# A softmax on one core: seven tiles of up to 31 rows in one written-out queue, in place of twelve of up to 15

## The chip, the cores and the metric

The kernel runs on one core of one Trainium2 chip. The metric is the device time of one execution in microseconds (us); the median of three runs is given. A profile belongs to one further execution, whose own time stands beside it.

## The reference

```python
x = np.random.randn(16, 1024, 512).astype(np.float32)

def reference(x):
    x_scaled = x / 2.0
    x_max = np.max(x_scaled, axis=-1, keepdims=True)
    exp_x = np.exp(x_scaled - x_max)
    return (exp_x / np.sum(exp_x, axis=-1, keepdims=True)).astype(np.float32)
```

A softmax with temperature 2 over the last axis of 512 values, for 16,384 vectors. 33.55 MB are read and 33.55 MB are written.

## The kernel before

The vectors are spread over the 128 partitions, so each partition has 128 vectors. In this document a *row* is one vector on each of the 128 partitions: 128 x 512 x 4 B = 262,144 B. There are 128 rows to load and 128 to store.

All data lives in one buffer in SBUF, `arena`, of 100 rows, and is worked on in place. `PLAN` (L11) lists the tiles: for each, the sizes of its chunks in rows and the place in the arena where it begins. A tile is the unit of transfer, a chunk the unit of computing. A tile of r rows is laid out so that each partition's share is contiguous in DRAM: one descriptor carries r x 2,048 B. Here there are 12 tiles of 3, 7, 15, 15, 15, 15, 15, 15, 15, 7, 3 and 3 rows; a tile of 15 rows has descriptors of 30,720 B and three chunks of 5 rows. The first eight tiles fill the arena (3 + 7 + 6 x 15 = 100 rows). The last four reuse places of earlier tiles, and `behind` (L63) lists for each which stores must have landed before it may be loaded.

Each chunk k goes through four steps:

- `do_max(k)` on VectorE (L86): the negated maximum of each vector, for the whole chunk in one instruction, once the tile's load has landed (`ld[t]`).
- ScalarE (L112): for each row one `activation`, exp of half the value plus the bias, with the sum of the vector as a second output.
- `do_mul(k)` on VectorE (L95, L99): the reciprocals of the sums in one instruction, and then one multiplication per row.
- `s_mul` counts the chunks that are finished, and a tile is stored when its last one is.

VectorE runs its instructions in the order written, which the loop at L125 sets: do_max(0), do_max(1), do_max(2), do_mul(0), do_max(3), do_mul(1), and so on, `LAG` = 2 chunks apart.

All transfers are issued by SyncE on one queue. `issue_loads` issues the eight loads that wait for nothing, two of them ahead of the start barrier of the program. Then SyncE stores tile after tile, waiting for `s_mul` at L133, and puts the four late loads between stores; these wait at L138 for the landing of the stores that they overwrite. At the end SyncE waits for every store (L141):

```python
        for t in range(len(tiles)):
            nc.sync.wait_ge(st[t], 16)
```

After that comes the closing barrier of all engines, with GpSimd gathering them. GpSimd itself has four small memsets at the start and no other work.

Of the kernel before, what the change touches and what calls it, by code (L numbers as in the profile page):

```python
# [1 line left out]

# [4 lines left out]

PLAN = [  # L11
    ([3], 0), ([4, 3], 3), ([5] * 3, 10), ([5] * 3, 25), ([5] * 3, 40), ([5] * 3, 55),
    ([5] * 3, 70), ([5] * 3, 85), ([5] * 3, 10), ([4, 3], 3), ([3], 0), ([3], 25),
]
ARENA = 100
LAG = 2


@with_exitstack
def kernel(  # L20
    ctx: ExitStack,
    tc: tile.TileContext,
    x: bass.AP,
    out: bass.AP,
):
    nc = tc.nc
    fp32 = mybir.dt.float32

    xf = x.flatten_outer_dims()
    of = out.flatten_outer_dims()  # L30
    N, D = xf.shape
    P = nc.NUM_PARTITIONS
    n_rows = N // P
    assert sum(sum(c) for c, _ in PLAN) == n_rows

    arena = nc.alloc_sbuf_tensor("arena", (P, ARENA, D), fp32)
    negmax = nc.alloc_sbuf_tensor("negmax", (P, n_rows), fp32)
    sums = nc.alloc_sbuf_tensor("sums", (P, n_rows), fp32)
    recip = nc.alloc_sbuf_tensor("recip", (P, n_rows), fp32)

    tiles, chunks, base = [], [], 0
    for t, (cs, at) in enumerate(PLAN):
        r = sum(cs)
        tiles.append((base, r, at))
        o = 0
        for c in cs:
            chunks.append((t, base + o, c, at + o))
            o += c  # L50
        base += r
    last_chunk = {c[0]: k for k, c in enumerate(chunks)}

    def dram(ap, t):
        b, r, _ = tiles[t]
        return ap[b * P : (b + r) * P].rearrange("(p r) d -> p r d", r=r)

    def sb(t):
        _, r, at = tiles[t]
        return arena[:, at : at + r, :]  # L60


    behind = {}  # L63
    for t, (_, r, at) in enumerate(tiles):
        for u in range(t):
            _, ru, au = tiles[u]
            if at < au + ru and au < at + r:
                behind.setdefault(t, []).append(u)

    ld = [tc.alloc_semaphore(f"ld{t}") for t in range(len(tiles))]  # L70
    st = [tc.alloc_semaphore(f"st{t}") for t in range(len(tiles))]
    s_max = tc.alloc_semaphore("s_max")
    s_exp = tc.alloc_semaphore("s_exp")
    s_rec = tc.alloc_semaphore("s_rec")
    s_mul = tc.alloc_semaphore("s_mul")

    def issue_loads(begin, end):
        for t in range(begin, end):  # L80
            if t not in behind:
                nc.sync.dma_start(out=sb(t), in_=dram(xf, t)).then_inc(ld[t], 16)

    def do_max(k):
        t, b, c, a = chunks[k]
        nc.vector.reduce_max(  # L86
            out=negmax[:, b : b + c],
            in_=arena[:, a : a + c],
            axis=mybir.AxisListType.X,
            negate=True,  # L90
        )._wait_ge(ld[t], 16).then_inc(s_max, 1)

    def do_mul(k):
        t, b, c, a = chunks[k]
        nc.vector.reciprocal(  # L95
            out=recip[:, b : b + c], in_=sums[:, b : b + c]
        )._wait_ge(s_exp, k + 1).then_inc(s_rec, 1)
        for r in range(c):
            ins = nc.vector.tensor_scalar_mul(  # L99
                out=arena[:, a + r],  # L100
                in0=arena[:, a + r],
                scalar1=recip[:, b + r : b + r + 1],
            )
            if r == 0:
                ins._wait_ge(s_rec, k + 1)
        ins.then_inc(s_mul, 1)

    def compute_and_store():

        for k, (t, b, c, a) in enumerate(chunks):  # L110
            for r in range(c):
                ins = nc.scalar.activation(  # L112
                    out=arena[:, a + r],
                    in_=arena[:, a + r],
                    func=mybir.ActivationFunctionType.Exp,
                    bias=negmax[:, b + r : b + r + 1],
                    scale=0.5,
                    accum_out=sums[:, b + r : b + r + 1],
                )
                if r == 0:  # L120
                    ins._wait_ge(s_max, k + 1)
            ins.then_inc(s_exp, 1)


        for k in range(len(chunks) + LAG):  # L125
            if k < len(chunks):
                do_max(k)
            if k >= LAG:
                do_mul(k - LAG)

        late = sorted(behind)
        for t in range(len(tiles)):
            nc.sync.wait_ge(s_mul, last_chunk[t] + 1)  # L133
            nc.sync.dma_start(out=dram(of, t), in_=sb(t)).then_inc(st[t], 16)
            while late and max(behind[late[0]]) <= t - 1:
                u = late.pop(0)
                for v in behind[u]:
                    nc.sync.wait_ge(st[v], 16)  # L138
                nc.sync.dma_start(out=sb(u), in_=dram(xf, u)).then_inc(ld[u], 16)
        for t in range(len(tiles)):  # L140
            nc.sync.wait_ge(st[t], 16)  # L141

    hook = nc.inst_callbacks[-1]
    nc.remove_inst_callback(hook)
    symbolic = nc._always_lower_symbolic_ap
    nc._always_lower_symbolic_ap = False
    here = str(nc.cur_bb)
    entry = nc.main_func.blocks[0]  # L150
    head, jumps = entry.instructions[:-5], entry.instructions[-5:]
    entry.instructions = []
    nc.switch_bb("main", None)
    issue_loads(0, 2)
    first = list(entry.instructions)
    at = next(k for k, i in enumerate(head) if type(i).__name__ == "InstDrain")
    entry.instructions = head[:at] + first + head[at:]
    issue_loads(2, len(tiles))
    compute_and_store()
    entry.instructions = list(entry.instructions) + jumps  # L160
    nc.switch_bb(here, None)
    nc._always_lower_symbolic_ap = symbolic
    nc.push_inst_callback(hook)


# [1 line left out]
_INS = ['x']  # L167
_OUTS = [((16, 1024, 512), 'float32')]


# [23 lines left out]
```

The softmax here doesn't subtract the row's maximum and nothing guards it: scores larger than these inputs give would overflow.

## Time and profile before

| what | value |
|---|---|
| median of 3 runs | 163.73 us (163.58 to 163.92) |
| profiled execution, its own time | 163.36 us |
| its span, first to last instruction | 161.6 us |
| VectorE busy | 126.1 us, until 137.9 us |
| ScalarE busy | 94.5 us |
| share of the 16 DMA engines | 97.7% of the span |
| moved | 67.14 MB, mean 416 GB/s |
| DMA packets of the kernel's queue | 3,456 |

The span is counted from the first instruction that the profiler records to the last; the execution's own time has some 1.8 us around it. The page gives the span in 40 slices of 4.04 us: a digit is the busy share of an engine in tenths, and the line of GB/s says what the DMA engines moved. The 3,456 packets are 24 transfers of 128 descriptors (3,072), and 16 small ones for each transfer (384), which count its landing up. A reduction in VectorE's timeline with "<-DMA" behind it stood waiting for a load, so that its start says when that load could be used.

### The profile page before, as it was taken

What the parts mean: (1) busy time and instruction counts of PE and PEld (TensorE: products, weight loads), DVE (VectorE), ACT (ScalarE), POOL (GpSimd) and SP (SyncE); (2) the same over time, 40 slices, a digit from 0 to 9 for tenths busy, and PEclk for the clock granted to TensorE, in tenths of its full rate; (3) what the DMA queues carried; (4) which work ended last, traced back from release to release, by engine and by line L of the source; (5) the groups of instructions that cost most, each with busy time, mean ns of one, the idle gap of its engine ahead of it and who ended that gap; (6) DMA issues with size and microseconds to landing.
All of it is one profiled execution on the core that took longest, in us unless ns stands there. A gap on an engine that the chain in (4) does not pass through costs nothing.

```text
span 161.6 us, 513 instructions
## 1 busy us (share of the span) xinstructions
DVE 126.1 (78%) x184; ACT 94.5 (59%) x257; POOL 0.2 (0%) x4
## 2 busy tenths in 40 slices
DVE  0484599999999999999999999999999999100000
ACT  3439087866688666797666886667978655000000
POOL 0000000000000000000000000000000000000000
DMA  7999999999999997999999899999999999999992
GB/s 291 465 403 449 441 418 464 395 458 395 464 411 436 449 411 254 444 438 472 418 434 464 388 431 406 445 456 388 461 441 456 395 464 395 464 411 456 390 410 90
DMA packets 3460, 67.14 MB, mean 416 GB/s; under 512 B 385, under 2 KB 385, under 8 KB 1153
## 3 DMA queue, kind: packets, MB, share of 16 engines
q1 hardware_dynamic: 3456, 67.11, 97.7%
q14 instruction: 4, 0.02, 0.0%
HBM read 33.55 MB, written 33.55 MB: 415 GB/s over the span
## 4 chain that ended last, share of the span: by engine, by line
DVE 74%; DMA 10%; issue 0%; DVEq 0%
DVE negmax L86 40%; DVE arena L99 32%; DMA arena<-in_x_dram 10%; DVE recip L95 2%; DVEq L189 0%
## 5 line engine op out<-in xcount | busy, mean ns | idle before, releaser
L112 ACT ACTIVATE arena<-arena,negmax 128x512 f32<-128x512 f32 x128 | 90.7, 710 | 40.1 <-DVE negmax L86 40.1
L86 DVE TENSOR_REDUCE negmax<-arena 128x5 f32<-128x2560 f32 (+2 forms) x28 | 72.3, 2586 | 10.8 <-DMA arena<-in_x_dram 10.8
L99 DVE TENSOR_SCALAR arena<-arena,recip 128x512 f32<-128x512 f32 x128 | 53.2, 482 | 1.0
L112 ACT ACTIVATION_READ_ACCUMULATOR arena<-arena,negmax 128x1 f32 x128 | 23.9, 187 | 0.0
L95 DVE RECIPROCAL recip<-sums 128x5 f32<-128x5 f32 (+2 forms) x28 | 5.0, 177 | 0.0
L112 ACT ACT_TABLE_LOAD x1 | 1.3, 1283 | 1.3 <-PEq L178 1.3
L178 POOL MEMSET const-bfloat16-1.0<- 128x1 bf16 x1 | 0.1, 101 | 0.0
L178 POOL MEMSET const-uint8-127<- 128x1 uint8 x1 | 0.1, 101 | 0.0
L178 POOL MEMSET const-float32-0.0<- 128x1 f32 x1 | 0.1, 98 | 0.2 <-issue 0.2
L178 POOL MEMSET const-float32-1.0<- 128x1 f32 x1 | 0.1, 98 | 0.0
## 6 DMA issues: line engine op xcount, KB each, us to landing
arena<-in_x_dram SPq DMA_DIRECT2D x7, 3840.0 KB, 33.7
out_dram<-arena SPq DMA_DIRECT2D x7, 3840.0 KB, 33.2
arena<-in_x_dram SPq DMA_DIRECT2D x2, 1792.0 KB, 15.2
out_dram<-arena SPq DMA_DIRECT2D x2, 1792.0 KB, 33.2
arena<-in_x_dram SPq DMA_DIRECT2D x3, 768.0 KB, 23.5
out_dram<-arena SPq DMA_DIRECT2D x3, 768.0 KB, 22.6
```

The source lines that it names most:

```text
L86: nc.vector.reduce_max(out=negmax[:, b : b + c], in_=arena[:, a : a + c], axis=mybir.AxisListType.X, negate=True,)._wait_ge(ld[t], 16).the ...
L95: nc.vector.reciprocal(out=recip[:, b : b + c], in_=sums[:, b : b + c])._wait_ge(s_exp, k + 1).then_inc(s_rec, 1)
L99: ins = nc.vector.tensor_scalar_mul(out=arena[:, a + r], in0=arena[:, a + r], scalar1=recip[:, b + r : b + r + 1],)
L112: ins = nc.scalar.activation(out=arena[:, a + r], in_=arena[:, a + r], func=mybir.ActivationFunctionType.Exp, bias=negmax[:, b + r : b + r ...
L178: nc = _bacc.Bacc("TRN2", target_bir_lowering=False, num_devices=1)
```

## The change

`PLAN` has seven tiles of 7, 15, 31, 31, 15, 22 and 7 rows, and 22 chunks of 3 to 8 rows in place of 28 of 3 to 5. The arena has 99 rows; the first five tiles fill it (7 + 15 + 31 + 31 + 15). A row share of 31 rows is a descriptor of 63,488 B. Tile 5 (22 rows) takes the places of tiles 0 and 1, tile 6 (7 rows) a part of that of tile 2.

The order of transfers is written out in `QUEUE`, and `do_queue` issues it on SyncE as it stands: a load waits for the stores in `behind`, a store for `s_mul`. Load 5 stands after store 2, load 6 after store 3. The first two loads (`EARLY`) go out ahead of the start barrier, as before.

Stores that a later load waits for (0, 1 and 2) keep a semaphore each; the others share `s_end`. The last wait is on GpSimd: four waits, for stores 0, 1, 2 and for `s_end`.

```diff
 PLAN = [
-    ([3], 0), ([4, 3], 3), ([5] * 3, 10), ([5] * 3, 25), ([5] * 3, 40), ([5] * 3, 55),
-    ([5] * 3, 70), ([5] * 3, 85), ([5] * 3, 10), ([4, 3], 3), ([3], 0), ([3], 25),
+    ([4, 3], 0), ([5] * 3, 7), ([8, 8, 8, 7], 22), ([8, 8, 8, 7], 53), ([5] * 3, 84),
+    ([6, 6, 5, 5], 0), ([4, 3], 22),
 ]
-ARENA = 100
+ARENA = 99
 LAG = 2
+QUEUE = [
+    ("load", 0), ("load", 1), ("load", 2), ("load", 3), ("load", 4),
+    ("store", 0), ("store", 1), ("store", 2), ("load", 5), ("store", 3), ("load", 6),
+    ("store", 4), ("store", 5),
+    ("store", 6),
+]
+EARLY = 2
...
+    awaited = {u for us in behind.values() for u in us}
...
-    st = [tc.alloc_semaphore(f"st{t}") for t in range(len(tiles))]
+    st = {t: tc.alloc_semaphore(f"st{t}") for t in sorted(awaited)}
+    s_end = tc.alloc_semaphore("s_end")
...
-    def issue_loads(begin, end):
-        for t in range(begin, end):
-            if t not in behind:
+    stored = {}
+
+    def do_queue(items):
+        for kind, t, *rest in items:
+            if kind == "load":
+                for u in behind.get(t, []):
+                    nc.sync.wait_ge(st[u], stored[u])
                 nc.sync.dma_start(out=sb(t), in_=dram(xf, t)).then_inc(ld[t], 16)
+                continue
+            lo, hi, groups = rest if rest else (0, tiles[t][1], [(0, P)])
+            b, r, at = tiles[t]
+            k = max(k for k, c in enumerate(chunks) if c[0] == t and c[1] - b < hi)
+            nc.sync.wait_ge(s_mul, k + 1)
+            for p, q in groups:
+                u = t if t in awaited else "end"
+                nc.sync.dma_start(
+                    out=dram(of, t)[p:q, lo:hi], in_=arena[p:q, at + lo : at + hi, :]
+                ).then_inc(st[t] if t in awaited else s_end, 16)
+                stored[u] = stored.get(u, 0) + 16
...
-        late = sorted(behind)
-        for t in range(len(tiles)):
-            nc.sync.wait_ge(s_mul, last_chunk[t] + 1)
-            nc.sync.dma_start(out=dram(of, t), in_=sb(t)).then_inc(st[t], 16)
-            while late and max(behind[late[0]]) <= t - 1:
-                u = late.pop(0)
-                for v in behind[u]:
-                    nc.sync.wait_ge(st[v], 16)
-                nc.sync.dma_start(out=sb(u), in_=dram(xf, u)).then_inc(ld[u], 16)
-        for t in range(len(tiles)):
-            nc.sync.wait_ge(st[t], 16)
...
-    issue_loads(0, 2)
+    do_queue(QUEUE[:EARLY])
...
-    issue_loads(2, len(tiles))
-    compute_and_store()
+    do_compute()
+    do_queue(QUEUE[EARLY:])
+
+    for u, sem in [*st.items(), ("end", s_end)]:
+        nc.gpsimd.wait_ge(sem, stored[u])
```

## The prediction

> **What bounds the kernel now.** I read the busy shares and slices of the page first, then the chain.
>
> ```profile
> DVE 126.1 (78%) x184; ACT 94.5 (59%) x257; POOL 0.2 (0%) x4
> ...
> DVE  0484599999999999999999999999999999100000
> ...
> DMA  7999999999999997999999899999999999999992
> GB/s 291 465 403 449 441 418 464 395 458 395 464 411 436 449 411 254 444 438 472 418 434 464 388 431 406 445 456 388 461 441 456 395 464 395 464 411 456 390 410 90
> ...
> q1 hardware_dynamic: 3456, 67.11, 97.7%
> ...
> DVE 74%; DMA 10%; issue 0%; DVEq 0%
> ```
>
> The chain names VectorE for 74%, but VectorE ends at 137.9 us of 161.6, and the last five slices show transfers alone. The queue is full at 97.7%: **bytes set the end**, and VectorE runs just ahead of them. The one hole is slice 16, with 254 GB/s. Windows give its size and the flow around it (columns: length, busy times of VectorE, ScalarE and GpSimd, clock, DMA share, GB/s):
>
> ```profile
> 0.00:1.00 1.00, 0.00 (x0) 0.00 (x0) 0.20 (x4) 1.00 0.00 0
> 1.00:2.00 1.00, 0.00 (x0) 0.74 (x1) 0.00 (x0) 1.00 0.92 264
> ```
>
> ```profile
> 60.00:64.00 4.00, 3.96 (x6) 2.71 (x9) 0.00 (x0) 1.00 0.80 238
> 64.00:100.00 36.00, 35.75 (x53) 26.95 (x75) 0.00 (x0) 1.00 1.01 434
> ```
>
> The hole costs (434 - 238) / 434 x 4 = 1.8 us. Next, the timeline of VectorE, where a reduction starts when its load is usable:
>
> ```profile
> 4.51 1.75 DVE L86 TENSOR_REDUCE negmax<-arena 128x3 f32<-128x1536 f32 x1 [4.51 <-DMA arena<-in_x_dram]
> 8.77 3.95 DVE L86 TENSOR_REDUCE negmax<-arena 128x4 f32<-128x2048 f32 x2 [2.51 <-DMA arena<-in_x_dram]
> 17.88 2.82 DVE L86 TENSOR_REDUCE negmax<-arena 128x5 f32<-128x2560 f32 x1 [3.77 <-DMA arena<-in_x_dram]
> ```
>
> Call a row of all 128 partitions (262,144 B) one row. These lines stand for 3, 10 and 25 rows: (17.88 - 8.77) / 15 = **0.607 us a row** in 30 KB descriptors, (8.77 - 4.51) / 7 = 0.609 in 14 KB ones. The first load took 4.51 - 3 x 0.607 = 2.7 us beside its bytes: 1.0 empty, about 0.4 of slow start (264 GB/s in the second microsecond), the rest landing.
>
> Last, the chain in order of time gives the prices of VectorE (start, us, what):
>
> ```profile
> 31.55 2.73 DVE negmax L86
> 34.27 0.11 DVE recip L95
> 34.38 0.02 issue
> 34.41 2.07 DVE arena L99 x5
> ...
> 120.28 2.19 DVE negmax L86
> ...
> 128.53 1.66 DVE negmax L86
> ...
> 133.77 1.28 DVE arena L99 x3
> ```
>
> A maximum over c rows costs 0.533c + 0.06 us (2.73, 2.19, 1.66 for 5, 4, 3); a scaling with its reciprocal 0.395c + 0.22 (2.20 for 5, 1.41 for 3). Together 0.93 us a row: slower than one transfer, quicker than a load and a store (1.21). So VectorE can't keep up while the queue only loads.
>
> **What the Trainium skill says.** "DMA: Bandwidth & Descriptors", section "Queues, rings and completion order": each DMA engine takes a queue's descriptors in ring order. The trace agrees: the store issued at 14.14 us landed 52.9 us later, behind all eight loads. Section "Where 436 GB/s comes from" puts the ceiling at 435.2 GB/s; 434 above is already there, so larger descriptors have nothing to win in the steady flow. Section "Latency and other measured facts" gives some 0.6 us to the first byte on this kind of queue; the trace has 1.0. No page prices a wait on GpSimd.
>
> **Part 1: descriptors.** Tiles fall from 12 to 7, transfers from 24 to 14. The 14 KB and 30 KB rows differ by 0.002 us. So I price a 62 KB row at 0.607 as well; the bounds are 0.604 (the ceiling) and 5% more, which no row excludes.
>
> **Part 2: the long tile delays VectorE.** Loads 0 to 4 go out at once, as before. Usable: load 0 (7 rows) at 4.51 + 4 x 0.607 = 6.9, load 1 (22 rows) at 8.77 + 12 x 0.607 = 16.1, load 2 (53 rows) at 8.77 + 43 x 0.607 = 34.9. VectorE works in order, and scalings come two chunks late (LAG). From 16.1: maxima of chunks 2, 3, 4 (3 x 2.73) and scalings of chunks 0, 1, 2 (1.80 + 1.41 + 2.20), 13.6 us, to 29.7. The maximum of chunk 5 waits for load 2, and the scalings of chunks 3 and 4, ready to run, stand behind it: 5.2 us idle. VectorE is idle for 5.7 + 5.2 + 5.2 us from 1.2 to 34.9, where before it was 10.8.
>
> **Part 3: store 2 comes too late.** Its wait is for the scaling of chunk 8, which stands after the maximum of chunk 10. From 34.9: maxima of 8, 8, 8, 7, 8, 8 rows = 5 x 4.32 + 3.79 = 25.4 us; scalings of 5, 5, 8, 8, 8, 7 rows = 2 x 2.20 + 3 x 3.38 + 2.99 = 17.5. Sum 42.9, so store 2 is issued at 77.8. ScalarE (5.7 us for 8 rows) has two maxima and a scaling as cover. Store 0 is issued about 25 and store 1 about 48, in time. The queue holds 99 loaded and 22 stored rows: 1.4 + 121 x 0.607 + 1.8 (the hole, if it comes again) = 76.7. Behind store 2 on SyncE stand load 5, store 3 and load 6, so nothing else can fill the queue. A restart costs 1.0 to 1.4 us by the first two windows; I take 1.2. First bytes at 79.0: **2.3 us empty**, 4.1 without the hole. Either way 79.0 holds, since VectorE sets it; here the hole costs nothing.
>
> **Part 4: the second stop.** From 79.0 run store 2, load 5, store 3, load 6: 91 rows, 55.2 us, to 134.2. Store 3's scaling is done at 77.8 + 26.7 = 104.5, before its turn at 79.0 + 53 x 0.607 = 111.2. Load 5 needs stores 0 and 1, load 6 needs store 2; they land long before those turns. Load 6 is usable at 134.2 + 1.1 = 135.3. VectorE, which works on load 5 from 112.3 for 21.7 us, is free at 134.0. Then maximum of 4 rows, scaling of 5, maximum of 3, scaling of 5: 2.28 + 2.20 + 1.66 + 2.20 = 8.3, so store 5 is issued at 143.7. The queue had store 4 (15 rows, 9.1 us) until 143.3. Store 5's bytes begin at 144.9: **1.6 us empty**. Store 6 is ready by 147 and hidden.
>
> **Part 5: the end.** Stores 5 and 6 are 29 rows, 17.6 us, to 162.5. In the kernel before, 1.4 + 256 x 0.607 + 1.8 = 158.6 us of flow stand against 160.5, where SyncE's last wait ended: 1.9 for landing and drift between the DMA engines. Drift restarts at each stop, so I take 0.8 (ends 0.4 and 1.9). From that wait to the end it was 161.6 - 160.5 = 1.1 us. The waits move to GpSimd, behind which nothing is queued but the closing barrier, and SyncE goes to the barrier early. That saves at most the 0.3 us in which SyncE's branch and drain passed; GpSimd could as well be slower by as much; I take -0.1. Span: 162.5 + 0.8 + 1.1 - 0.1 = **164.3**. Semaphores and instructions fall in number, which costs or saves nothing seen.
>
> **Sum.** The profiled execution was 163.36 us, 1.8 beside its 161.6 span, and 0.37 below the median of 163.73. The new span gives 164.3 + 1.8 + 0.4 = **166.5 us**, +2.8.
>
> **Rivals.**
> - **More loss:** 62 KB descriptors cost 5% more, or the hole comes after the first stop. On the path lie 31 long rows before 34.9 and 62 after 79.0, 93 x 0.607 = 56.5 us; 5% is 2.8, the hole 1.8. For it: the hole's cause isn't shown. Against: descriptor size didn't matter from 14 to 30 KB. 168.3 to 169.3.
> - **Cheaper restarts:** 0.6 us each and landings shorter by 0.3, with the barrier's full gain: 166.5 - 1.7 = 164.8. Against: the second at the start shows 1.0.
> - **Faster:** long descriptors lift the rate itself. The 56.5 us would have to fall by 3.2 us, 5.6%, for a gain over 0.3: 0.573 us a row, or 457 GB/s. The windows and the ceiling speak against it. At 6%, 163.1.
> - **It does not do what it says:** a 63,488 B row is cut in two. Then rates are those of 30 KB rows and both stops stay: 166.5.
>
> **Numbers.** Forecast (with the cut rows) 0.68, more loss 0.20, cheaper restarts 0.08, faster 0.04. The forecast itself is good for 165.3 to 167.7. The range reaches from the cheap restarts to the hole uncovered and some drift, 164.8 to 168.8. A measurement here tells about 0.2% (0.33 us) from no change: faster 0.04, same 0.03 (the cheapest restarts with luck), slower 0.93.
>
> **What would show it.** Packets 14 x 144 = 2016 if rows aren't cut. Slices of the DMA near 77 to 79 and 143 to 145 us dip; VectorE waits three times until 34.9, then about 2.7 near 112 and 1.3 near 135; the first reduction of 8 rows starts at 34.9. SyncE's issues of store 2 near 77.8 and store 5 near 143.7. It is wrong if the queue never empties, if VectorE's pace is other than 0.93 us a row, or if rows of the long tiles take other than 0.607 us.

## The result, and the profile after

The changed kernel takes 168.27 us (median of 4 runs, 167.93 to 168.74); the kernel before, on the same chip, 163.66 us. The ratio is 1.0283, 95% interval 1.0254 to 1.0313: slower by 4.6 us. The forecast was 166.5 with a range of 164.8 to 168.8: the time lies in the range, but above the 165.3 to 167.7 that the forecast itself was good for. The profiled execution took 168.27 us, with a span of 166.5.

The page of the changed kernel, busy shares, slices and queue:

```profile
DVE 124.9 (75%) x172; ACT 93.9 (56%) x257; POOL 0.2 (0%) x4
...
DVE  0270999259999999999999999944999978990000
...
DMA  7999998999989999991999699999989899889985
...
q1 hardware_dynamic: 2016, 67.11, 95.8%
...
DVE 49%; DMA 40%; issue 0%; DVEq 0%; SPq 0%
```

The packets are 2,016 = 14 x 144, so a row of 63,488 B goes as one descriptor. The digit 1 in the line of the DMA, slice 19 (74.9 to 79.1 us), is a queue that was empty. Before, no slice but the last stood under 7. The timeline of VectorE shows five waits for loads, three of them before 36 us, as forecast:

```profile
7.41 3.95 DVE L108 TENSOR_REDUCE negmax<-arena 128x4 f32<-128x2048 f32 x2 [7.41 <-DMA arena<-in_x_dram]
...
16.51 2.82 DVE L108 TENSOR_REDUCE negmax<-arena 128x5 f32<-128x2560 f32 x1 [5.15 <-DMA arena<-in_x_dram]
...
35.26 4.42 DVE L108 TENSOR_REDUCE negmax<-arena 128x8 f32<-128x4096 f32 x1 [5.09 <-DMA arena<-in_x_dram]
...
114.58 3.35 DVE L108 TENSOR_REDUCE negmax<-arena 128x6 f32<-128x3072 f32 x1 [4.45 <-DMA arena<-in_x_dram]
...
138.06 2.29 DVE L108 TENSOR_REDUCE negmax<-arena 128x4 f32<-128x2048 f32 x1 [1.80 <-DMA arena<-in_x_dram]
```

The timeline of SyncE has the two stores on which the queue waited (start, us, what). The store of 78.44 is store 2; the first of the pair at 146.45 is store 5:

```profile
78.44 0.33 SPq L101 DMA_DIRECT2D out_dram<-arena  x1
78.88 0.36 SPq L93 DMA_DIRECT2D arena<-in_x_dram  x1
```

```profile
146.45 3.52 SPq L101 DMA_DIRECT2D out_dram<-arena  x2
```

And windows of one microsecond show both stops (the last two columns are the DMA share and GB/s):

```profile
76.00:77.00 1.00, 1.00 (x4) 1.00 (x5) 0.00 (x0) 1.00 0.15 61
77.00:78.00 1.00, 1.00 (x4) 1.00 (x3) 0.00 (x0) 1.00 0.00 0
78.00:79.00 1.00, 1.00 (x3) 1.00 (x5) 0.00 (x0) 1.00 0.00 0
79.00:80.00 1.00, 1.00 (x1) 1.00 (x4) 0.00 (x0) 1.00 2.40 1016
80.00:81.00 1.00, 1.00 (x1) 1.00 (x3) 0.00 (x0) 1.00 0.00 0
...
145.00:146.00 1.00, 1.00 (x4) 1.00 (x4) 0.00 (x0) 1.00 0.22 92
146.00:147.00 1.00, 0.96 (x5) 0.47 (x2) 0.00 (x0) 1.00 0.00 0
```

The lines of 79 and 80 us show how to read such a window: it counts each packet whole, in the window in which the packet starts. At 79 us all 16 engines start a packet of 63,488 B (16 x 63,488 B = 1.016 MB), they take 2.40 us on average, and so none starts in the next window. Windows much longer than a packet tell two losses apart. Where the share falls well below 1, engines stand empty. Where GB/s falls and the share doesn't, the engines are busy and the packets take longer. The time lost in this second way is length x (share - GB/s / 434), with the flow of 434 GB/s from before; a packet on a window's edge moves both columns alike and drops out.

| step | forecast | measured |
|---|---|---|
| load 2 usable | 34.9 | 35.26 |
| store 2 issued | 77.8 | 78.44 |
| load 5 usable | 112.3 | 114.58 |
| load 6 usable | 135.3 | 138.06 |
| store 5 issued | 143.7 | 146.45 |
| span | 164.3 | 166.5 |

The mechanism is the one forecast; 2.2 us of size are missing. Store 2 came 0.6 us late, and the end ran 0.5 us shorter than forecast. The 2.1 us between arise from the issue of store 2 to the use of load 6: 57.5 us were forecast, 59.6 measured. The most of it is in the first 53 rows (store 2 and load 5), where 114.58 - 78.44 = 36.1 stand against 34.5. So the experiments ask two things: are the two stops the loss, and what else costs time behind them?

### The profile page after: what moved, and what is told of

It is laid out like the page before. It is cut to its first block, busy times and chain, and to the rows that moved or that the text cites. A ratio compares the mean times of both kernels' runs of the same rounds, so it can differ in the third digit from the quotient of the medians.

```text
span 166.5 us, 488 instructions
## 1 busy us (share of the span) xinstructions
DVE 124.9 (75%) x172; ACT 93.9 (56%) x257; POOL 0.2 (0%) x4
## 3 DMA queue, kind: packets, MB, share of 16 engines
q1 hardware_dynamic: 2016, 67.11, 95.8%
## 4 chain that ended last, share of the span: by engine, by line
DVE 49%; DMA 40%; issue 0%; DVEq 0%; SPq 0%
DMA arena<-in_x_dram 40%; DVE negmax L108 26%; DVE arena L121 22%; DVE recip L117 1%; DVEq L202 0%; SPq L101 0%
## 5 line engine op out<-in xcount | busy, mean ns | idle before, releaser
L108 DVE TENSOR_REDUCE negmax<-arena 128x5 f32<-128x2560 f32 (+5 forms) x22 | 71.4, 3251 | 23.9 <-DMA arena<-in_x_dram 23.9
L117 DVE RECIPROCAL recip<-sums 128x5 f32<-128x5 f32 (+5 forms) x22 | 4.0, 183 | 0.0
## 6 DMA issues: line engine op xcount, KB each, us to landing
arena<-in_x_dram SPq DMA_DIRECT2D x2, 7936.0 KB, 43.2
```

Of the source, the lines that this page charges most:

```text
L108: nc.vector.reduce_max(out=negmax[:, b : b + c], in_=arena[:, a : a + c], axis=mybir.AxisListType.X, negate=True,)._wait_ge(ld[t], 16).the ...
L117: nc.vector.reciprocal(out=recip[:, b : b + c], in_=sums[:, b : b + c])._wait_ge(s_exp, k + 1).then_inc(s_rec, 1)
```

## The experiments

Each is an edit of the changed kernel, unless another is named. The kernel before ran beside each of them. Three chips were used for them. The median of the kernel before was 163.52 us on the chip of the first four experiments, 163.03 on that of the copies with 15 and 7 rows, the copy with a stop and the last experiment, and 163.15 on that of the copy with 31 rows and the small load. So the ratios are what compares across chips.

**The old tiles in the new queue.**

```diff
-    ([4, 3], 0), ([5] * 3, 7), ([8, 8, 8, 7], 22), ...
+    ([3], 0), ([4, 3], 3), ([5] * 3, 10), ...    # PLAN and the order of transfers as before
```

> The twelve tiles of before in the same order of transfers, but issued by do_queue, with shared s_end and GpSimd waiting at the end. Theory (tile sizes and order alone make the loss): 163.6 us, within 0.2% of before; the stretch from the last wait to the end is shorter by 0.1 us at most. Rival (part of the loss is the new waiting on GpSimd or the single semaphore): 164.5 us or more, and the closing stretch longer than 1.1 us.

Measured: 163.53 us against 163.52, ratio 1.0003 (0.9986 to 1.0019). In the profile GpSimd's branch comes at 161.0 and the span ends at 162.0; with SyncE waiting the branch came at 160.6 and the end at 161.6. So the wait on GpSimd, the shared semaphore and `do_queue` cost and save nothing that can be told (the interval is 0.2% to either side), and the loss lies in tile sizes and order.

**Store 2 alone in two halves.**

```diff
-    ("store", 2),
+    ("store", 2, 0, 16, [(0, 128)]), ("store", 2, 16, 31, [(0, 128)]),
```

> The changed kernel, with store 2 alone cut in two (rows 0 to 15 and 16 to 31 of the tile), so that its first half can go when chunk 6 is done, about 63 us; the loads and VectorE's late start stay. Theory (store 2, issued as one at 78.4, empties the queue): the hole at 76 to 79 us is gone, store 3 and load 6 come about 3 us earlier, 164.8 us (-3.5). The second stop at about 142 stays. Rival (VectorE's late start itself sets the end): 168.3 us, or the stop returns elsewhere. Side question: store 2 now ends in 30 KB descriptors ahead of load 5; if long descriptors make the hole at that turn (about 0.9 us at 95 to 99 in the changed kernel), that one shrinks too.

Measured: 163.96 us, ratio 1.0028 (1.0014 to 1.0042), 0.8 us better than the forecast of it. The first stop is gone; the windows of this kernel at 76 us and at its second stop:

```profile
76.00:80.00 4.00, 4.00 (x8) 4.00 (x13) 0.00 (x0) 1.00 1.10 474
```

```profile
140.00:141.00 1.00, 0.96 (x4) 1.00 (x3) 0.00 (x0) 1.00 0.36 154
141.00:142.00 1.00, 1.00 (x3) 1.00 (x4) 0.00 (x0) 1.00 0.22 92
142.00:143.00 1.00, 0.96 (x4) 0.18 (x2) 0.00 (x0) 1.00 0.53 225
```

How the extra gain came is seen on load 5, from the table of DMA issues, first of the changed kernel and then of this one (last column: us to landing):

```profile
arena<-in_x_dram SPq DMA_DIRECT2D x1, 5632.0 KB, 35.7
```

```profile
arena<-in_x_dram SPq DMA_DIRECT2D x1, 5632.0 KB, 31.1
```

Issued at 78.88 and 79.16, it was there at 114.6 and at 110.3: 4.3 us apart. The stop itself is 2.9 of that (the time for which the 16 engines were empty between 75.8 and 79.5 us, by the starts and lengths of the packets). The rest was lost behind the stop, at two turns of the queue. Windows of the changed kernel at the turn from store 2 to load 5, and at that from load 5 to store 3:

```profile
93.00:102.00 9.00, 8.96 (x12) 5.65 (x16) 0.00 (x0) 1.00 0.99 386
108.00:118.00 10.00, 5.52 (x8) 3.63 (x11) 0.00 (x0) 1.00 1.02 398
```

The first lost 9 x (0.99 - 386 / 434) = 0.9 us, the second 10 x (1.02 - 398 / 434) = 1.0 us, both with the engines busy. The last packets of store 2 show it directly: the 16 of the second line take 3.11 us on average, where those of the line before took 2.35. Stop and turns together are 0.5 more than the 4.3: a landing shows the slowest engine, the windows the mean of the 16.

```profile
93.00:94.00 1.00, 1.00 (x2) 1.00 (x3) 0.00 (x0) 1.00 2.35 1016
95.00:96.00 1.00, 1.00 (x2) 0.01 (x1) 0.00 (x0) 1.00 3.11 1016
```

With store 2 in halves the same turns, at nearly the same times, cost next to nothing (0.1 us at most):

```profile
93.00:102.00 9.00, 8.96 (x13) 5.93 (x18) 0.00 (x0) 1.00 1.05 451
108.00:114.00 6.00, 5.93 (x10) 3.94 (x11) 0.00 (x0) 1.00 1.12 484
```

The side question stays open here: the loss at 95 to 99 us is gone, but the stop and the 62 KB descriptors of store 2 went together.

**Tile 2 as two tiles, load and store.**

```diff
-    ([8, 8, 8, 7], 22), ([8, 8, 8, 7], 53), ...
+    ([8, 8], 22), ([8, 7], 38), ([8, 8, 8, 7], 53), ...    # and QUEUE with one load and store more
```

> The changed kernel with tile 2 cut into tiles of 16 and 15 rows, load and store: VectorE no longer waits until 35.3 for its third load. Theory (one cause, the indivisible store): no better than cutting the store alone, 164.8 us; VectorE waits 2 times instead of 3 in the first 36 us, and that gain is not on the path. Rival (VectorE's lost 5 us count by themselves): at least 1 us faster than with the store alone cut, 163.5 us or less.

Measured: 163.73 us, ratio 1.0011 (0.9998 to 1.0025). VectorE waits twice in the first 36 us, has its work 5 us earlier, and the end moves by 0.23 us, within the intervals of the two. So VectorE's late start harms through store 2 alone, as far as these intervals tell.

**Load 6 ahead of store 3.**

```diff
-    ("store", 2), ("load", 5), ("store", 3), ("load", 6),
+    ("store", 2), ("load", 5), ("load", 6), ("store", 3),
```

> The changed kernel with load 6 moved ahead of store 3 in the queue. Theory: load 6 is usable some 18 us earlier, VectorE never waits for it, the second stop (145.3 to 147.3) goes: -1.6 us; and the queue changes direction twice less, with the load of 14 KB descriptors at the turn instead of the 44 KB one, worth another 0.7 to 1.0: 165.8 us. Rival (turns cost nothing by themselves, the holes come by the clock): -1.6 alone, 166.7 us, with a hole at 108 to 114 us as before. Second rival (the stop just moves to store 4 or 5): 168 us.

Measured: 166.66 us, ratio 1.0186 (1.0161 to 1.0211), 1.6 less than the changed kernel. The second stop is gone, and is worth what was forecast; the gain expected from fewer turns did not come. Load 5, no longer last before the turn to stores, landed 34.5 us after its issue, 1.2 earlier, but the loss moved on to load 6, with its 14 KB descriptors. Windows of this kernel at the turn from store 2 to load 5, and at that from load 6 to store 3:

```profile
93.00:102.00 9.00, 8.96 (x12) 5.61 (x16) 0.00 (x0) 1.00 0.99 386
112.00:120.00 8.00, 6.60 (x8) 3.24 (x9) 0.00 (x0) 1.00 1.11 428
```

They lost 0.9 and 8 x (1.11 - 428 / 434) = 1.0 us, as in the changed kernel. So the length of the descriptors at a turn is not what makes it dear, as I had thought. The time is the rival's 166.7, but the hole that it put at 108 to 114 us isn't there (102 to 112 us reads a share of 1.00 and 433 GB/s): it moved with the turn.

**Transfers alone.** Three copies without computing: a store waits for its load, nothing else.

```diff
-            nc.sync.wait_ge(s_mul, k + 1)
+            nc.sync.wait_ge(ld[t], 16)
...
-    do_compute()
```

> Transfers alone: nothing is computed, the input is copied to the output in tiles of 15 rows, in the order L0 L1 L2 S0 L3 S1 L4 S2 L5 S3 L6 S4 L7 S5 L8 S6 S7 S8, so the queue changes direction 12 times (6 to stores) and never empties. Theory (a turn costs about 1 us only while the 16 DMA engines are in step, and spreads them; later turns are cheap): 1.4 + 256 x 0.606 and one or two holes, span 159 to 160 us, holes only at the first turns (28 to 37 us), none later. Rival (every turn to stores costs 1.1 us at 30 KB): six times, span 165 us or more.

Measured, one run: 164.26 us, span 162.5, between the two. (The order has 13 changes of direction, 7 of them to stores, one more than the expectation counted.) Windows of this kernel; the first turn to stores is near 28 us (GpSimd alone has a busy column here):

```profile
4.00:24.00 20.00, 0.00 (x0) 1.00 1.00 432
24.00:32.00 8.00, 0.00 (x0) 1.00 1.00 369
...
70.00:150.00 80.00, 0.00 (x0) 1.00 1.01 433
```

(432 - 369) / 432 x 8 = 1.2 us went at the first turn, and the flow over the four later turns to stores after 70 us is flat. A load has landed when the slowest of the 16 DMA engines has done its part, and for that one the landings (issue time and time to landing added) tell a little more. Load 2 was there at 30.0 us, and loads 3 to 8 at 49.8, 68.6, 87.5, 105.7, 124.5 and 138.4. At 0.607 us a row, these intervals hold 1.6, 0.6, 0.7, 0.0, 0.6 and -0.1 us too much. So the engines together lose next to nothing at later turns, while the slowest one falls behind, and that shows at the end:

```profile
158.00:160.00 2.00, 0.00 (x0) 1.00 0.19 82
```

Most engines have finished here, but the last packet ends at 161.1 us. This uneven end makes up the most of the 2.5 us over the 160 expected. Whether turns set the slowest engine back isn't shown.

```diff
     ("store", 3),
+    ("drain", 32),     # SyncE waits until stores 2 and 3 have landed
     ("load", 6),
```

> The copy of c15_copy, with SyncE waiting after store 3 until stores 2 and 3 have landed, so that the queue empties once (near 95 us) and starts again with all engines together. Theory (in step again, so the next turns cost again): the stop itself some 2 us, and new holes of about 1 us at the next one or two turns, 3 to 4 us more than c15_copy, less up to 2 where the engines' spread at the stop is part of the stop. Rival (holes come by the first use of a direction, or by the clock): only the stop, +1.5 to 2.0, the flow after it flat at 433 GB/s.

Measured, one run: 168.68 us, 4.4 more than without the stop, a little above the 3 to 4 expected. Windows of this kernel:

```profile
70.00:92.00 22.00, 0.00 (x0) 1.00 1.01 434
92.00:100.00 8.00, 0.00 (x0) 1.00 0.50 180
100.00:104.00 4.00, 0.00 (x0) 1.00 0.98 422
104.00:110.00 6.00, 0.00 (x0) 1.00 1.01 338
110.00:124.00 14.00, 0.00 (x0) 1.00 1.01 437
124.00:130.00 6.00, 0.00 (x0) 1.00 0.97 420
```

The stop itself left the engines empty for some 8 x (1 - 0.50) = 4 us, twice what was expected, so the total says little; the flow behind the stop is what decides. After 100 us it is up again, and then it has a hole at 104 to 110, 6 x (1.01 - 338 / 434) = 1.4 us, at the first turn to stores behind the stop. The next such turn, at 124 to 130, has nearly none. Load 6, issued into the empty queue, took 13.3 us to land with a turn behind it; the very first load of the same size, into an empty queue too but with loads behind it, took 11.9. So the first turn to stores is dear again **after a stop**. That the hole comes at a set time, or once in a program, is out.

> The copy with tiles of 7 rows (14 KB descriptors), 34 changes of direction. Theory: as c15_copy, plus some 0.3 us for more descriptors, span 159.5 to 160.5 us. Rival (each turn costs by its descriptor, 0.3 us at 14 KB): 17 turns to stores, 5 us more, span 164 us or more.

Measured, one run: 164.66 us, span 162.9. Windows of this kernel:

```profile
4.00:12.00 8.00, 0.00 (x0) 1.00 1.01 430
12.00:18.00 6.00, 0.00 (x0) 1.00 1.00 351
18.00:60.00 42.00, 0.00 (x0) 1.00 1.01 427
60.00:150.00 90.00, 0.00 (x0) 1.00 1.01 430
```

Again one hole, (430 - 351) / 430 x 6 = 1.1 us, at the first turn. With 33 turns (17 to stores) the span is only 0.4 us over that of c15_copy, and above the 159.5 to 160.5 expected. A price of 0.3 us for each turn to stores, some ten of them from 60 to 150 us, would lower the flow there by 3%; it is the same 430 GB/s as ahead of the first turn. So a price per turn by descriptor length is out.

> The copy with tiles of 31 rows: 62 KB descriptors nearly throughout, 7 changes of direction. Theory (descriptor size costs nothing in the flow; only the first turn to stores has a hole): span 161 to 163 us, as c15_copy (162.5) and c7_copy (162.9). Rival (62 KB descriptors run 3 to 5% slower, the surplus of the changed kernel): span 167 to 170 us.

Measured, one run: 162.41 us, span 160.6, the shortest of the copies and just below the 161 to 163 expected. Descriptors of 62 KB are not slower; the rival that priced them at 3 to 5% falls. That they are faster isn't shown, since this copy also has the fewest turns.

**A small load at the first turn.** The old tiles in the new queue, the eighth cut:

```diff
-    ([5] * 3, 85),
+    ([5, 4, 3], 85), ([3], 97),
```

> The old plan in the new queue (as e1_old_plan), with the eighth tile cut into 12 and 3 rows, so that the first turn to stores, near 60 us, comes behind a load with 6 KB descriptors instead of 30 KB. Theory now (the first turn after an empty queue costs about 1 us whatever its descriptors, since load 6 with 14 KB cost it in e6_load6_early): the hole at 60 to 64 us stays at 1.0 us or more, 163.5 us. Rival (the last load's long descriptors make the hole): it falls below 0.3 us, and the time to 162.5 us.

Measured: 163.48 us, ratio 1.0010 (0.9994 to 1.0027). The window of this kernel at the turn:

```profile
60.00:64.00 4.00, 3.96 (x6) 2.71 (x9) 0.00 (x0) 1.00 0.95 275
```

The hole stays, 4 x (0.95 - 275 / 434) = 1.3 us, with 6 KB descriptors in the last load. The kernel before lost as much; its window of 60 to 64 us cuts the hole short, and a wider one holds it all, 8 x (0.94 - 335 / 434) = 1.3 us:

```profile
58.00:66.00 8.00, 7.93 (x15) 5.75 (x16) 0.00 (x0) 1.00 0.94 335
```

**Neither stop.** Store 2 in halves and load 6 ahead of store 3, both edits above together.

> The changed kernel without either stop: store 2 cut in two and load 6 ahead of store 3. Theory (the stops and the turns behind them are the whole loss): below store 2 cut alone (163.96) by its remaining stop of 2.0 us, so 162.0 to 162.5 us, at or under the kernel before; holes only at the first turn near 60 us. Rival (the long tiles cost something besides): 163.5 us or more.

Measured: 162.62 us against 163.03 for the kernel before, ratio 0.9978 (0.9966 to 0.9989): faster than both kernels, and the rival falls. The gain is smaller than expected, though. The expectation took its 163.96 us from another chip; by the ratios, removing the second stop as well is worth 1.0028 - 0.9978 = 0.50%, 0.8 us, where 2.0 were expected. Some loss is left near 140 us, where store 5 is still a little late; where the rest of the difference lies isn't shown. The windows of this kernel:

```profile
58.00:64.00 6.00, 5.96 (x11) 4.55 (x15) 0.00 (x0) 1.00 0.99 342
64.00:76.00 12.00, 11.93 (x13) 7.34 (x21) 0.00 (x0) 1.00 1.01 435
...
138.00:144.00 6.00, 5.35 (x16) 2.23 (x6) 0.00 (x0) 1.00 0.93 399
```

The hole of the first turn at 58 to 64 is there, as in every kernel, the last window holds an empty stretch of 6 x (1 - 0.93) = 0.4 us, and the rest of the loss against the kernel before is gone.

## Why the prediction was right, and where it was short

- **What bounds the kernel** was right: bytes, with VectorE close behind. VectorE's pace held: store 2 was issued 43.2 us after load 2 could be used, against 42.9.
- **Part 1, descriptors:** right. The copy with 62 KB rows is no slower than those with 14 and 30 KB, and a round of 62 KB packets in 2.35 us is 432 GB/s. The ceiling of 435.2 GB/s that the Trainium skill gives ("DMA: Bandwidth & Descriptors", section "Where 436 GB/s comes from") fits: the long undisturbed windows above read 427 to 437, where 437 over 14 us is no more than the counting of packets at a window's edges.
- **Parts 2 and 3, the first stop:** right in cause and place. The cut of store 2 alone brings the ratio from 1.0283 to 1.0028. Its price was short: 2.3 us empty were counted and 2.9 came, and its removal is worth 2.55% of 163.66 us, 4.2 us.
- **Part 4, the second stop:** 1.6 us empty were forecast, and moving load 6 takes off 0.97%, 1.6 us. The two removals together take off 3.05%, 5.0 us, less than 4.2 + 1.6: with the first stop gone, the second removal brings 0.8 us only.
- **Part 4, the flow between the stops, is the term that failed.** It took 91 rows at 0.607 us, 55.2 us, as flat, and counted the hole of 60 us as one event that the stop covers. Such holes come at the first turns behind an empty queue, so the stop brought them back, on the path and uncovered: 0.9 us from store 2 to load 5 and 1.0 from load 5 to store 3. In the landings, the first 53 rows after the stop lost 1.7 us against the flat price, and the next 38 another 0.4 (138.06 - 114.58 = 23.5, less 38 x 0.607 = 23.1).
- **Part 5, the end:** from the issue of store 5 to the end 20.6 us were forecast and 20.05 came. That the drift between the DMA engines starts anew at a stop was right: at the end of the changed kernel their last packets land within 0.2 us of each other, in the kernel before over some 2 us. GpSimd's wait was worth nothing measurable.
- **The rivals:** "more loss" named the hole after the first stop and its 168.3 us, which is where the time fell, 168.27. That the figure fits so well is luck: its 1.8 us came from the window of 60 to 64 us with the share of 0.80 overlooked, where the hole is 1.3 us, and two slow turns came behind the stop, not one. Its other half, dearer long descriptors, was wrong. Its weight of 0.20 was too small: the profile before shows a hole exactly where the queue turns from loads to stores, and I called its cause open instead of asking when it would come again.

What stays open is why the first turn is dear. The copies show when it comes. The expectations put it down to DMA engines that run in step and are spread by the turn. In the changed kernel all 16 do start their packets together after the stop (the windows of 79 and 80 us). But ahead of the first turn of c15_copy the starts of 16 successive packets, by the trace, lay 0.91 us apart, most of a packet's 1.14 us, and that turn was dear as well. So starting together isn't needed for it, and no run tests any other sense of "in step". Nor does any run take the turn from stores to loads by itself.

## What to carry to other kernels

When transfers set the end, a transfer that can't be issued until late stops the queue for all that is queued behind it; look for the last instruction that each one waits for, and cut that transfer rather than all of them. A stop costs more than its empty time: here 1 to 2 us more at the turns of the queue behind it. Larger descriptors had little to win once 14 KB ones ran at full rate. The seven tiles were faster than the twelve, by 0.2%, only after both stops were gone or nearly so; which part of the change brings that gain isn't shown. In a profile, look at the share and the GB/s together: an empty queue lowers both, a slow turn the GB/s alone.

## What the runs showed of the hardware

The first turn from loads to stores after the queue had been empty cost 1.0 to 1.4 us in every kernel whose windows are shown here at that turn, with the engines busy and the packets slower. Last loads with descriptors of 6, 14, 30 and 44 KB made little difference. A turn from stores to loads right behind a stop cost 0.9 us. Later turns to stores left the flow of the 16 engines together flat (433 GB/s over 80 us), while the landings of the slowest engine came 0 to 0.7 us later than the flat price between one load and the next. In undisturbed flow a row took 0.609 us in 14 KB descriptors, 0.607 in 30 KB ones, and 0.606 in 62 KB ones (8 packets of 2.35 us on each engine for 31 rows).
